# Entry of layer 1: queries and first keys built tile by tile of the contraction, values ahead of the context's keys, norms placed anew

## The chip, the cores and the metric

One core of a Trainium2 chip runs the whole forward pass as one program. The metric is the device time of one execution in microseconds (us). Three runs of the kernel before took 1241.14, 1241.52 and 1244.07 us; the median is 1241.52.

TensorE (PE) multiplies, VectorE (DVE) and ScalarE (ACT) work on tiles, GpSimd (POOL) takes small element-wise work, and the queue of SyncE (SP) issues nearly all DMAs.

## The reference, cut to what matters

Two layers act on 256 latent and 256 context tokens of width 1024. Layer 0 is retention, layer 1 differential attention; each ends in a gated feed-forward net. Every sublayer starts with an RMS norm whose result is scaled and shifted by vectors computed from a condition ("adaLN"). In the last layer only the latent tokens are wanted, so layer 1 forms queries for latents alone, but keys and values for both streams.

```python
h = rms_norm(x) * (1.0 + scale) + shift          # for latents and for context
q, k, v = split(h @ w_in)                        # width 1024 each, 8 heads x 2 x 64
q, k = rms_norm_gain(q), rms_norm_gain(k)        # over each 64; rope_2d on the latents' only
s = q @ k.T / 8                                  # two score maps m per head
p = softmax(s[m=0]) - lam * softmax(s[m=1])
o = rms_norm_gain(p @ v) * (1 - lambda_init)     # over each 128
x = x + gate * (o @ w_out)
```

All of it is float32.

## The kernel before

**Streams.** `xs[m]`, `hh[m]`, `hl[m]` hold feature tile m (128 features, m = 0 to 7) of all 512 tokens: columns 0 to 255 are the context (`CTX`), 256 to 511 the latents (`LAT`). Every float32 product is done as three products of a high and a low part in the rounded type `fp32r` (`mm3`, L106): high x high, high x low, low x high. `split` (L102) makes the parts: ACT copies to the high one, DVE subtracts to the low one. Weights are loaded and split by `load_w` (L113) in pieces of 128 x 1024; each of the rings `raw`, `whi`, `wlo` has five buffers. One load of 1024 rows by 256 columns is two such pieces, contraction tiles 0 to 3 and 4 to 7.

**Order.** Each engine runs its instructions in one fixed order. The framework fixes it when the program is built: among what it expects to be ready by its own costs, the instruction written first goes first, so a matmul written later can be put ahead of one whose operands it expects late. Two lists place work in the written order. `after(n, fn)` (L70) runs `fn` at the n-th coming `step()`, and `acc()` (L83), which hands out one of four accumulator banks, begins with a `step()`. In layer 1 `defer(n, fn)` (L755) runs `fn` at the n-th coming `tick()`; a tick stands behind each half projection (24 matmuls of 128 x 256).

**End of layer 0.** `ffn_out` (L675) adds the last part of the feed-forward net: eight blocks of 12 matmuls for the latents, then eight for the context. `gated_add` (L308) adds each block to `xs` on DVE, ACT squares the result, and POOL adds the square to a running sum (`norm_square`, L272). The sum over features is then taken by four small matmuls, and DVE and POOL form the inverse root (`norm`, L291). Its `spread` brings the root to all partitions by matmuls against `ones` (L249), and `modulate` (L257) makes `hh`, `hl`: per tile one DVE instruction, one on ACT and one more on DVE. `NB` and `NS` (L42, L44) say how many steps later the norm and its spread are run: for the latents 0 and 6, for the context 0 and 0. The context's are thus written ahead of the first query matmul, in the `acc()` of that projection.

**Layer 1.** Four groups g of two heads (`diff_group`, L816). The written order of group 0 is: queries of the latents, keys of the latents, keys of the context, values of the latents (token tiles 2, 3), values of the context (0, 1). `proj_pair` (L767) forms 128 tokens x 256 columns of one token tile over all eight contraction tiles, then the next token tile, both in one bank. `qk_pair` (L778) squares on ACT, sums on DVE, takes the root on POOL, multiplies by it, and applies gain and rope on DVE. Transposes on PE (`q_transpose`, `k_transpose`) are deferred by `PQK` ticks; the tile of scores (`scores`), the transposed probabilities (`probs`) and the products with the values (`values`) by `SC0` + `STEP0` in group 0 and `SC` + `STEP` in groups 1 and 2. The scores have two banks of their own (tag `sc`, one buffer of two banks), the transposes two (tag `tp`).

Of the kernel before, what the change touches and what calls it, by code (L numbers as in the profile page):

```python
# [11 lines left out]
F32 = mybir.dt.float32  # L12
F32R = mybir.dt.float32r
AF = mybir.ActivationFunctionType
ALU = mybir.AluOpType
AX = mybir.AxisListType

P = 128
# [32 lines left out]
def hybrid_trunk(ctx: ExitStack, tc: tile.TileContext, xt_in, cols_in, ada_first, ada_wt, c, c_ctx, ret_w_in,  # L51
# [18 lines left out]
    def after(n, fn):  # L70
        queue.append([n, fn])
# [219 lines left out]
    def norm(layer, which, half, a, later):  # L291
        nm = f"{layer}_{which}_{half.start}"
        ps = tps(f"ms_{nm}")
        for i in range(2):
            T.matmul(ps[:, 2 * i:2 * i + 2], a[:, i * P:(i + 1) * P], mean_col, start=True, stop=True)
        rc = small.tile([P, 2], F32, tag="rc", name=f"rc_{nm}")
        V.tensor_copy(rc, ps[:, 0:4:2])
        rsqrt(rc)

        def spread():  # L300
            r, = spread_rows(rc, nm)
            for m in range(KT):
                modulate(layer, which, m, half, r)
            fresh[half.start] = (layer, which)

        after(later, spread)

    def gated_add(layer, ch, m, half, ps):  # L308
        s = 0 if half == CTX else 1
# [221 lines left out]
    for h in range(NH0):  # L531
        us = [None] * 4

        def u_hook(i):
            for j in range(4):
                if UP[j] == i:
                    us[j] = ret_u(h - 1, j, pend[0], pend[1][j])

        q, k, *sgs = ret_first() if h == 0 else ret_qk(h, u_hook)
        if h == 0:  # L540
            V.tensor_scalar(out=lw[:, 4], in0=lw[:, 3], scalar1=2.0, scalar2=None, op0=ALU.add)
            V.reciprocal(lw[:, 5], lw[:, 4])
            V.tensor_tensor(out=lw[:, 4], in0=lw[:, 3], in1=lw[:, 5], op=ALU.mult)
            V.tensor_tensor(out=lw[:, 5], in0=lw[:, 4], in1=lw[:, 4], op=ALU.mult)
            V.tensor_scalar(out=lw[:, 6], in0=lw[:, 5], scalar1=1.0 / 19, scalar2=1.0 / 17, op0=ALU.mult, op1=ALU.add)
            for kk in (15, 13, 11, 9, 7, 5, 3, 1):
                V.tensor_tensor(out=lw[:, 6], in0=lw[:, 6], in1=lw[:, 5], op=ALU.mult)
                V.tensor_scalar(out=lw[:, 6], in0=lw[:, 6], scalar1=1.0 / kk, scalar2=None, op0=ALU.add)
            V.tensor_tensor(out=lw[:, 6], in0=lw[:, 6], in1=lw[:, 4], op=ALU.mult)
            V.tensor_scalar(out=lw[:, 7], in0=lgt, scalar1=0.0, scalar2=None, op0=ALU.min)  # L550
            V.scalar_tensor_tensor(out=lg, in0=lw[:, 6], scalar=-2.0, in1=lw[:, 7], op0=ALU.mult, op1=ALU.add)

            lgn = loc.tile([P, 8], F32, name="lgn")
            V.tensor_scalar(out=lgn, in0=lg, scalar1=float(NL), scalar2=None, op0=ALU.mult)
            lneg = loc.tile([P, 8], F32, name="lneg")
            V.tensor_scalar(out=lneg, in0=lg, scalar1=-1.0, scalar2=None, op0=ALU.mult)
            lam4 = scratch("lam4")[:, :4 * DH].rearrange("p (a d) -> p a d", a=4)
            nc.sync.dma_start(lam4.rearrange("p a d -> p (a d)"),
                              diff_lambda.rearrange("o a d -> o (a d)").broadcast_to([P, 4 * DH]))
            lam = const.tile([P, 8], F32, name="lam")  # L560
            lv = scratch("lv")[:, :2 * DH].rearrange("p (a d) -> p a d", a=2)
            V.tensor_tensor(out=lv[:, 0], in0=lam4[:, 0], in1=lam4[:, 1], op=ALU.mult)
            V.tensor_tensor(out=lv[:, 1], in0=lam4[:, 2], in1=lam4[:, 3], op=ALU.mult)
            V.tensor_reduce(out=lam[:, 0:2], in_=lv, op=ALU.add, axis=AX.X)
            S.activation(lam[:, 2:4], lam[:, 0:2], AF.Exp)
            V.tensor_tensor(out=lam[:, 4:5], in0=lam[:, 3:4], in1=lam[:, 2:3], op=ALU.subtract)
            V.tensor_scalar(out=lam[:, 5:6], in0=lam[:, 4:5], scalar1=-LAMBDA_INIT, scalar2=None, op0=ALU.add)
            neg_lam = lam[:, 5:6]
            fs = decay_tables(0)
        if pend is not None:  # L570
            ret_out(h - 1, us, [ALL])
        pt = ret_scores(h, q, k, fs)
        vs = ret_v(h)
        sgs = sgs[0] if sgs else ret_g(h, 0)
        os = ret_av(h, pt, vs)
        if h + 1 < NH0:
            fs = decay_tables(h + 1)
        us = [None] * 4

        def u_last(i):  # L580
            for j in range(4):
                if UL[j] == i:
                    us[j] = ret_u(h, j, os, (sgs + done)[j])

        done = []
        sgs += ret_g(h, 1, u_last if h == NH0 - 1 else None, done)
        pend = (os, sgs)
    ret_out(NH0 - 1, us, [CTX, LAT])

    def ffn_in(layer, g0, g1, first):  # L590
# [84 lines left out]
    def ffn_out(layer, g0, g1, us, done=None):  # L675
# [14 lines left out]
        if layer == 0:  # L690
            for half in ([LAT, CTX] if g1 == 4 else [ALL]):
                n = half.stop - half.start
                a = None
                for m in range(KT):
                    ps = acc(f"fo_{layer}_{g0}_{m}_{half.start}")
                    mm3(ps[:, :n], [wv(m, k) + (us[k][0][:, half], us[k][1][:, half]) for k in range(g1)])
                    if n == NT:
                        gated_add(0, 5, m, CTX, ps[:, CTX])
                        gated_add(0, 5, m, LAT, ps[:, LAT])
                    else:  # L700
                        gated_add(0, 5, m, half, ps[:, :n])
                        a = norm_square(1, 0, half, m, a)
                if n == NL:
                    after(NB[2 + (half == CTX)], lambda half=half, a=a: norm(1, 0, half, a, NS[2 + (half == CTX)]))
        else:
            for m0 in range(0, KT, 2):
                ps = acc(f"fo_{layer}_{g0}_{m0}")
                for m in (m0, m0 + 1):
                    mm3(ps[:, (m - m0) * NL:(m - m0 + 1) * NL], [wv(m, k) + us[k] for k in range(g1)])
                for m in (m0, m0 + 1):  # L710
                    gated_add(1, 5, m, LAT, ps[:, (m - m0) * NL:(m - m0 + 1) * NL])
                    if done is not None:
                        done(m)
# [61 lines left out]
                tick()  # L775
        return ps

    def qk_pair(w, wt, t0, name):  # L778
        ps = proj_pair(wt, t0, name)
        sq = scratch(f"sq_{name}")  # L780
        S.activation(sq, ps, AF.Square)
        ss = small.tile([P, 8], F32, tag="ss", name=f"ss_{name}")
        V.tensor_reduce(out=ss, in_=sq.rearrange("p (g i) -> p g i", g=8), op=ALU.add, axis=AX.X)
        rsqrt(ss, EPS * DH)
        n = loc.tile([P, 512], F32, tag="qkn", name=f"n_{name}", bufs=2)
        nv = n.rearrange("p (g i) -> p g i", g=8)
        V.tensor_tensor(out=nv, in0=ps.rearrange("p (g i) -> p g i", g=8),
                        in1=ss.unsqueeze(2).broadcast_to([P, 8, DH]), op=ALU.mult)
        o = loc.tile([P, 512], F32, tag="qko", name=f"o_{name}", bufs=2)
        if t0 < 2:  # L790
            V.tensor_tensor(out=o.rearrange("p (g i) -> p g i", g=8), in0=nv,
# [24 lines left out]
    def diff_group(g):  # L816
# [27 lines left out]
                V.tensor_tensor(out=k2[m][b, :, dst], in0=tv[a], in1=k2[m][a, :, dst].bitcast(F32), op=ALU.subtract)  # L844
            st["k", t0] = k2

        qo = qk_pair(0, wq, 2, f"q_{g}")
        tick()
        defer(PQK[0 if g else 2], lambda: q_transpose(qo))
        for t0 in (2, 0):  # L850
            ko = qk_pair(1, wk, t0, f"k_{g}_{t0}")
            tick()
            defer(PQK[1 if g else 3 + (t0 == 0)], lambda t0=t0, ko=ko: k_transpose(t0, ko))
        wv = load_w(wi1[:, 2048 + g * 256:2048 + (g + 1) * 256], KT, 256, f"dv_{g}")
        v = loc.tile([P, 4, 256], F32, tag="v1", name=f"v1_{g}", bufs=2)

# [50 lines left out]
        def heads_out():  # L907
# [8 lines left out]
                                   op0=ALU.mult, op1=ALU.subtract)  # L916
            st["out"] = (hi, lo)

        for n, (i, h) in enumerate(((0, 0), (0, 1), (1, 0), (1, 1))):
            at = (SC0 if g == 0 else SC if g < 3 else SC3)[n]  # L920
            for k, fn in enumerate((scores, probs, values)):
                defer(at + (STEP0 if g == 0 else STEP if g < 3 else STEP3)[k], lambda fn=fn, i=i, h=h: fn(i, h))
        defer((HO if g < 3 else HO3)[0], heads_out)
        for n in range(4):
            defer((HO if g < 3 else HO3)[1 + n], lambda n=n: diff_out(g, st, 2 * n))
        def value_half(t):
            if t % 2 == 0:
                st["vps", t // 2] = acc(f"ps_dv_{g}_{t}")
            ts, half = slice(t * P, (t + 1) * P), slice((t % 2) * 256, (t % 2 + 1) * 256)
            ps = st["vps", t // 2]  # L930
            mm3(ps[:, half], [(hh[k][:, ts], hl[k][:, ts], wv[0][k], wv[1][k]) for k in range(KT)])
            if t % 2:
                S.activation(v[:, t - 1:t + 1].rearrange("p t n -> p (t n)"), ps, AF.Copy)
                st["v", t // 2] = v

        for n, t in enumerate((2, 3, 0, 1)):
            if g < 3:
                value_half(t)
                tick()
            else:  # L940
                defer(V3[n], lambda t=t: value_half(t))
# [108 lines left out]
```

## Time and profile before

| | |
|---|---|
| median of three runs | 1241.52 us |
| profiled execution, its own time | 1245.21 us |
| its span, first to last instruction | 1243.4 us |
| mean granted share of PE's clock | 0.995 |
| PE busy | 1207.1 us, 97% |
| weight loads into PE | 1045.8 us, 84% |
| DVE busy | 852.5 us, 69% |
| ACT busy | 471.0 us, 38% |
| POOL busy | 84.3 us, 7% |
| HBM read | 174.14 MB, 141 GB/s over the span |
| chain that ended last, by engine | PE 84%, DVE 8%, POOL 3%, ACT 2%, issue 2%, DMA 1% |

The profile is of one execution. Busy time counts the instructions of an engine from start to end; PE's overlap one another, and a row with `[idle before <-releaser]` says how long the engine stood still and what it then waited for. In names, buffer numbers are left out: `ps_q`, `ps_k`, `ps_dv` are the projections of layer 1, `sqa` the running sum of squares, `ms` its sum over features, `rb` the spread root, `qtp`, `ktp`, `ptp` transposes of queries, keys and probabilities, `dsc` scores.

### The profile page before, as it was taken

Reading aid. Unit: us, or ns where it says so; the run is one execution under the profiler, and the core shown is the slowest. Engines: PE = TensorE matmul, PEld = TensorE weight load, DVE = VectorE, ACT = ScalarE, POOL = GpSimd, SP = SyncE. Lnnn points to the kernel's source line nnn. Section 1 sums busy time; section 2 is a strip of 40 time slices with the busy share of each in tenths; the row PEclk is TensorE's granted clock in tenths of the full one; section 3 lists DMA queues with packets and bytes.
Section 4 is the critical chain, followed back from the end, with each engine's and each line's share of the span. In section 5 each row is a group of like instructions: output and inputs, shape, how many; then the busy total and the mean of one; then the engine's idle time right before and its main releaser. Section 6 shows DMA issues by size and latency. Waiting matters only on the chain.

```text
span 1243.4 us, 18122 instructions
## 1 busy us (share of the span) xinstructions
PE 1207.1 (97%) x7136; PEld 1045.8 (84%) x7136; DVE 852.5 (69%) x1483; ACT 471.0 (38%) x756; POOL 84.3 (7%) x87
## 2 busy tenths in 40 slices
PE   6999999999999999999999999999899998999998
PEld 5677778878788788888888888888899998999998
DVE  3479896688597579976575543348787788855555
ACT  3253323224232235323222312225565566644442
POOL 0000000000000032000000000012212112000000
PEclk9999999999999999999999999999999999999999
DMA  9724455245344332766576532232222413657563
GB/s 315 269 83 128 154 161 156 82 125 155 95 124 156 98 105 70 236 206 193 180 234 187 165 123 76 94 102 86 85 87 68 119 35 102 181 183 212 158 184 102
DMA packets 127509, 176.36 MB, mean 142 GB/s; under 512 B 6721, under 2 KB 100417, under 8 KB 127425
## 3 DMA queue, kind: packets, MB, share of 16 engines
q1 hardware_dynamic: 126272, 174.42, 45.2%
q8 instruction: 56, 0.92, 0.3%
q10 hardware_dynamic: 1152, 0.79, 0.2%
q14 instruction: 29, 0.23, 0.1%
HBM read 174.14 MB, written 1.05 MB: 141 GB/s over the span
## 4 chain that ended last, share of the span: by engine, by line
PE 84%; DVE 8%; POOL 3%; ACT 2%; issue 2%; DMA 1%; POOLq 0%; ACTq 0%; DVEq 0%
PE fo L111 5%; PE fo L110 5%; PE fo L109 5%; PE fpg L111 5%; PE fpg L109 5%; PE fpg L110 5%; PE fpa L111 5%; PE fpa L109 5%; PE fpa L110 5%; PE vps L109 2%; PE vps L111 2%; PE vps L110 2%; PE gps L110 2%; PE gps L111 2%; PE gps L109 2%; PE qkps L109 2%
## 5 line engine op out<-in xcount | busy, mean ns | idle before, releaser
L230 DVE CUSTOM_DVE_ANT_0 junk<-adaw,silb,biasx 128x1024 bf16<-128x1024 f32 x128 | 165.1, 1290 | 58.4 <-DMA adaw<-in_ada_wt_dram 57.7
L109 PE MATMUL fo<-fuh,whi_fo 128*128 128x256 f32 (+1 forms) x352 | 115.1, 327 | 0.0
L110 PE MATMUL fo<-ful,whi_fo 128*128 128x256 f32 (+1 forms) x352 | 114.9, 326 | 0.0
L111 PE MATMUL fo<-fuh,wlo_fo 128*128 128x256 f32 (+1 forms) x352 | 114.9, 326 | 0.0
L104 DVE TENSOR_TENSOR wlo_fo<-raw_fo,whi_fo 128x1024 fp32r<-128x1024 f32 (+1 forms) x56 | 55.6, 994 | 59.5 <-ACT whi_fo L103 59.4
L103 ACT ACTIVATE whi_fo<-raw_fo 128x1024 fp32r<-128x1024 f32 (+1 forms) x56 | 49.1, 878 | 113.5 <-PE fo L110 62.3
L109 PE MATMUL fpa<-hh,whi_fa 128*128 128x512 f32 (+1 forms) x192 | 72.6, 378 | 1.1 <-ACT hh L266 1.1
L110 PE MATMUL fpg<-hl,whi_fg 128*128 128x512 f32 (+1 forms) x192 | 72.6, 378 | 0.0
L109 PE MATMUL fpg<-hh,whi_fg 128*128 128x512 f32 (+1 forms) x192 | 72.5, 378 | 0.0
L110 PE MATMUL fpa<-hl,whi_fa 128*128 128x512 f32 (+1 forms) x192 | 72.5, 378 | 0.0
L111 PE MATMUL fpa<-hh,wlo_fa 128*128 128x512 f32 (+1 forms) x192 | 72.5, 377 | 0.0
L111 PE MATMUL fpg<-hh,wlo_fg 128*128 128x512 f32 (+1 forms) x192 | 72.4, 377 | 0.0
L109 PEld LDWEIGHTS fo<-fuh,whi_fo 128*128 128x128 f32 x352 | 66.1, 188 | 6.7
L110 PEld LDWEIGHTS fo<-ful,whi_fo 128*128 128x128 f32 x352 | 66.1, 188 | 6.7
L111 PEld LDWEIGHTS fo<-fuh,wlo_fo 128*128 128x128 f32 x352 | 66.1, 188 | 6.6
L311 DVE SCALAR_TENSOR_TENSOR x<-fo,mod,x 128x256 f32<-128x256 f32 x96 | 42.8, 479 | 40.7 <-PE fo L111 40.7
L104 DVE TENSOR_TENSOR wlo_fg<-raw_fg,whi_fg 128x1024 fp32r<-128x1024 f32 x40 | 49.0, 1226 | 29.9 <-ACT whi_fg L103 29.9
L279 POOL TENSOR_TENSOR sqa<-sqa,sq 128x256 f32<-128x256 f32 x35 | 35.6, 1017 | 396.2 <-issue 346.9
L103 ACT ACTIVATE whi_fa<-raw_fa 128x1024 fp32r<-128x1024 f32 x40 | 42.3, 1057 | 51.9 <-PE fo L110 18.9
L104 DVE TENSOR_TENSOR wlo_fa<-raw_fa,whi_fa 128x1024 fp32r<-128x1024 f32 x40 | 48.7, 1221 | 17.2 <-ACT whi_fa L103 16.7
L103 ACT ACTIVATE whi_fg<-raw_fg 128x1024 fp32r<-128x1024 f32 x40 | 42.4, 1060 | 45.0 <-issue 14.7
L109 PE MATMUL ops<-uh,whi_wo 128*128 128x512 f32 (+1 forms) x160 | 56.4, 364 | 1.4 <-ACT uh L103 1.1
(315 smaller groups left out, 3475.3 us busy)
## 6 DMA issues: line engine op xcount, KB each, us to landing
adaw<-in_ada_wt_dram SPq DMA_DIRECT2D x80, 512.0 KB, 3.7
raw_fa<-in_ffn_w_in_dram SPq DMA_DIRECT2D x40, 512.0 KB, 3.6
raw_fg<-in_ffn_w_in_dram SPq DMA_DIRECT2D x40, 512.0 KB, 4.3
raw_fo<-in_ffn_w_out_dram SPq DMA_DIRECT2D x32, 512.0 KB, 3.5
ada<-in_ada_first_dram SPq DMA_DIRECT2D x32, 256.0 KB, 5.4
raw_v<-in_ret_w_in_dram SPq DMA_DIRECT2D x16, 512.0 KB, 3.7
raw_wo<-in_ret_w_out_dram SPq DMA_DIRECT2D x16, 512.0 KB, 3.8
raw_g<-in_ret_w_in_dram SPq DMA_DIRECT2D x14, 512.0 KB, 3.6
```

Source lines behind the costliest of these rows:

```text
L103: S.activation(hi, src, AF.Copy)
L104: (eng or V).tensor_tensor(out=lo, in0=src, in1=hi.bitcast(F32), op=ALU.subtract)
L109: T.matmul(out_ps, ah, bh, start=(first and i == 0), stop=False)
L110: T.matmul(out_ps, ah, bl, start=False, stop=False)
L111: T.matmul(out_ps, al, bh, start=False, stop=(last and i == n - 1))
L230: V.tensor_tensor_reduce(out=junk, in0=raw, in1=silb[:, s], scale=1.0, scalar=biasx[:, b:b + 1], op0=ALU.mult, op1=ALU.add, accum_out=mod[ ...
L279: G.tensor_tensor(out=a, in0=a, in1=sq, op=ALU.add)
L311: V.scalar_tensor_tensor(out=xs[m][:, half], in0=ps, scalar=mod[:, layer, ch, s, m:m + 1], in1=xs[m][:, half], op0=ALU.mult, op1=ALU.add)
```

## The change

The opening of group 0 goes over the contraction tiles outermost: for each k three products, queries of token tile 2, queries of tile 3, first keys of tile 2, in three banks (the queries' two are the score banks). The context's norm is written into step 3 and its spread into step 6 of that loop. The second half of the latent keys follows, then the latent values, then the context's keys, and only then are the scores deferred. At the end of layer 0 the latents' norm and its spread are now run 2 and 2 steps later.

```diff
@@ norm
-        after(later, spread)
+        if isinstance(later, dict):
+            later["spread"] = spread
+        else:
+            after(later, spread)
@@ ahead of ret_out of the last head
+    sq0 = [None]
     ret_out(NH0 - 1, us, [CTX, LAT])
@@ ffn_out, layer 0
-                if n == NL:
-                    after(NB[2 + (half == CTX)], lambda half=half, a=a: norm(1, 0, half, a, NS[2 + (half == CTX)]))
+                if n == NL and half == LAT:
+                    after(2, lambda half=half, a=a: norm(1, 0, half, a, 2))
+                elif n == NL:
+                    sq0.append(a)
@@ layer 1
-    def qk_pair(w, wt, t0, name):
-        ps = proj_pair(wt, t0, name)
+    chain = {}
+
+    def opening(wq, wk):
+        ps = apsum.tile([P, 2, 512], F32, tag="sc", name="ps_q_open")
+        pk = acc("ps_k_open")
+        need(1, 0, LAT)
+        for k in range(KT):
+            if k == 3:
+                norm(1, 0, CTX, sq0[1], chain)
+            if k == 6:
+                chain["spread"]()
+            for o, t, w in ((ps[:, 0, :256], 2, wq), (ps[:, 1, :256], 3, wq), (pk[:, :256], 2, wk)):
+                ts = slice(t * P, (t + 1) * P)
+                mm3(o, [(hh[k][:, ts], hl[k][:, ts], w[0][k], w[1][k])], k == 0, k == KT - 1)
+        tick()
+        return ps[:, :, :256], pk
+
+    def opening_key(pk, wk):
+        ts = slice(3 * P, 4 * P)
+        mm3(pk[:, 256:], [(hh[k][:, ts], hl[k][:, ts], wk[0][k], wk[1][k]) for k in range(KT)])
+        tick()
+        return pk
+
+    def qk_pair(w, wt, t0, name, ps=None):
+        ps = proj_pair(wt, t0, name) if ps is None else ps
...
@@ diff_group
-        qo = qk_pair(0, wq, 2, f"q_{g}")
+        pq, pk = (None, None) if g else opening(wq, wk)
+        qo = qk_pair(0, wq, 2, f"q_{g}", pq)
         tick()
         defer(PQK[0 if g else 2], lambda: q_transpose(qo))
-        for t0 in (2, 0):
-            ko = qk_pair(1, wk, t0, f"k_{g}_{t0}")
+        ko = qk_pair(1, wk, 2, f"k_{g}_2", None if g else opening_key(pk, wk))
+        tick()
+        defer(PQK[1 if g else 3], lambda ko=ko: k_transpose(2, ko))
+
+        def context_keys():
+            ko = qk_pair(1, wk, 0, f"k_{g}_0")
             tick()
-            defer(PQK[1 if g else 3 + (t0 == 0)], lambda t0=t0, ko=ko: k_transpose(t0, ko))
+            defer(PQK[1 if g else 4], lambda: k_transpose(0, ko))
+
+        if g:
+            context_keys()
...
+        if g == 0:
+            for t in (2, 3):
+                value_half(t)
+                tick()
+            context_keys()
         for n, (i, h) in enumerate(((0, 0), (0, 1), (1, 0), (1, 1))):
             at = (SC0 if g == 0 else SC if g < 3 else SC3)[n]
...
-        for n, t in enumerate((2, 3, 0, 1)):
+        for n, t in enumerate((2, 3, 0, 1) if g else (0, 1)):
             if g < 3:
                 value_half(t)
                 tick()
```

In `qk_pair` the squares and the products with the root read the queries of group 0 from two banks through views of one more dimension; `value_half` moves up unchanged, with a check of its operands.

## Rows read from the trace of the kernel before

**Rows 1.** Windows: us, busy us (instructions) by engine, PE clock, DMA share, GB/s.

```profile
850.20:861.00 10.80, 8.44 (x62) 7.42 (x60) 9.56 (x22) 5.80 (x11) 3.01 (x3) 1.00 0.29 89
861.00:875.62 14.62, 13.77 (x111) 13.54 (x112) 12.89 (x31) 8.52 (x15) 2.54 (x1) 1.00 0.35 108
875.62:889.10 13.48, 10.69 (x87) 10.32 (x88) 10.64 (x20) 7.00 (x11) 4.18 (x2) 1.00 0.25 79
889.10:928.50 39.40, 38.87 (x310) 37.78 (x309) 34.14 (x58) 24.25 (x50) 6.49 (x4) 1.00 0.28 81
```

**Rows 2.** Waits of PE, 850.2 to 863: waited for, total, times, longest us.

```profile
PE ps_q L109 <- ACT hh L266: 0.9, 2, 0.5
```

**Rows 3.** Timeline of PE, 838 to 905: start, length, instruction, times, idle before.

```profile
839.37 0.61 PE L295 MATMUL ms<-mean_col,sqa 128*128 128x2 f32 x4 [0.56 <-POOL sqa L279]
...
846.98 0.59 PE L249 MATMUL rb<-dg,ones 128*128 128x256 f32 x2
...
851.73 0.28 PE L109 MATMUL ps_k<-whi_dk,hh 128*128 128x256 f32 x1
...
856.23 0.28 PE L110 MATMUL ps_q<-wlo_dq,hh 128*128 128x256 f32 x1
857.72 0.61 PE L295 MATMUL ms<-mean_col,sqa 128*128 128x2 f32 x4 [1.21 <-POOL sqa L279]
...
861.10 0.70 PE L249 MATMUL rb<-dg,ones 128*128 128x256 f32 x2 [0.27 <-DVE dg L246]
```

**Rows 4.** Waits of PE, 863 to 892.

```profile
PE ktp L813 <- DVE o_k L805: 1.5, 1, 1.5
PE ktp L813 <- DVE ql L833: 1.3, 1, 1.3
PE qtp L813 <- issue: 0.8, 1, 0.8
```

**Rows 5.** Window in layer 1's first feed-forward stage, four banks; PE alone.

```profile
1066.00:1078.00 12.00, 12.00 (x102) 1.00 0.36 110
```

**Rows 6.** Groups of DVE, 843.9 to 858: times, busy us, mean ns, idle before.

```profile
L265 DVE SCALAR_TENSOR_TENSOR n<-x,mod,r 128x256 f32<-128x256 f32 x8 | 4.0, 546 | 0.0
L267 DVE SCALAR_TENSOR_TENSOR hl<-n,mod,hh 128x256 fp32r<-128x256 f32 x8 | 3.9, 531 | 0.0
...
L311 DVE SCALAR_TENSOR_TENSOR x<-fo,mod,x 128x256 f32<-128x256 f32 x5 | 2.4, 476 | 0.9 <-PE fo L111 0.9
```

**Rows 7.** Timeline of DVE, 838 to 905.

```profile
848.43 1.84 DVE L265 SCALAR_TENSOR_TENSOR n<-x,mod,r 128x256 f32<-128x256 f32 x3
...
855.34 0.47 DVE L311 SCALAR_TENSOR_TENSOR x<-fo,mod,x 128x256 f32<-128x256 f32 x1
...
857.01 0.94 DVE L267 SCALAR_TENSOR_TENSOR hl<-n,mod,hh 128x256 fp32r<-128x256 f32 x1
...
861.60 1.23 DVE L104 TENSOR_TENSOR wlo_dv<-raw_dv,whi_dv 128x1024 fp32r<-128x1024 f32 x1 [0.56 <-ACT whi_dv L103]
```

**Rows 8.** Timeline of POOL, 838 to 905.

```profile
838.59 0.72 POOL L279 TENSOR_TENSOR sqa<-sqa,sq 128x256 f32<-128x256 f32 x1 [0.66 <-ACT sq L277]
...
856.49 1.18 POOL L279 TENSOR_TENSOR sqa<-sqa,sq 128x256 f32<-128x256 f32 x1 [0.48 <-ACT sq L277]
```

**Rows 9.** Timeline of ACT, 838 to 905.

```profile
860.51 1.06 ACT L103 ACTIVATE whi_dv<-raw_dv 128x1024 fp32r<-128x1024 f32 x1 [4.17 <-PE ps_q L111]
...
895.63 0.20 ACT L871 ACTIVATION_READ_ACCUMULATOR p<-dsc,mx 128x1 f32 x1
```

**Rows 10.** Timeline of DVE, the first keys' chain.

```profile
878.26 0.69 DVE L787 TENSOR_TENSOR n_k<-ps_k,ss_k 128x512 f32<-128x512 f32 x1 [1.53 <-POOL ss_k L143]
```

**Rows 11.** Timeline of PE at scores and transposed probabilities.

```profile
892.00 0.39 PE L864 MATMUL dsc<-k,qh 128*128 128x512 f32 x1
...
945.17 0.63 PE L881 MATMUL ptp<-ident,pf 128*128 128x128 f32 x4 [0.96 <-DVE pf L874]
...
992.47 0.63 PE L881 MATMUL ptp<-ident,pf 128*128 128x128 f32 x4 [1.86 <-DVE pf L874]
```

More of the change, by code (lines that the diff above doesn't have):

```diff
@@ L776, in proj_pair @@
         return ps
-    def qk_pair(w, wt, t0, name):
-        ps = proj_pair(wt, t0, name)
-        sq = scratch(f"sq_{name}")
-        S.activation(sq, ps, AF.Square)
+    chain = {}
[20 more added lines that the diff above has]
+        ps = proj_pair(wt, t0, name) if ps is None else ps
+        sq = scratch(f"sq_{name}")
+        if len(ps.shape) == 3:
+            S.activation(sq.rearrange("p (t n) -> p t n", t=2), ps, AF.Square)
+            ps = ps.rearrange("p t (g i) -> p t g i", g=4)
+        else:
+            S.activation(sq, ps, AF.Square)
+            ps = ps.rearrange("p (t g i) -> p t g i", t=2, g=4)
         ss = small.tile([P, 8], F32, tag="ss", name=f"ss_{name}")
@@ L786, in qk_pair @@
         nv = n.rearrange("p (g i) -> p g i", g=8)
-        V.tensor_tensor(out=nv, in0=ps.rearrange("p (g i) -> p g i", g=8),
-                        in1=ss.unsqueeze(2).broadcast_to([P, 8, DH]), op=ALU.mult)
+        V.tensor_tensor(out=n.rearrange("p (t g i) -> p t g i", t=2, g=4), in0=ps,
+                        in1=ss.rearrange("p (t g) -> p t g", t=2).unsqueeze(3).broadcast_to([P, 2, 4, DH]), op=ALU.mult)
         o = loc.tile([P, 512], F32, tag="qko", name=f"o_{name}", bufs=2)
@@ L917, in heads_out, with value_half @@
             st["out"] = (hi, lo)
+        def value_half(t):
+            if t % 2 == 0:
+                st["vps", t // 2] = acc(f"ps_dv_{g}_{t}")
+            ts, half = slice(t * P, (t + 1) * P), slice((t % 2) * 256, (t % 2 + 1) * 256)
+            ps = st["vps", t // 2]
+            need(1, 0, LAT if t >= 2 else CTX)
+            mm3(ps[:, half], [(hh[k][:, ts], hl[k][:, ts], wv[0][k], wv[1][k]) for k in range(KT)])
+            if t % 2:
+                S.activation(v[:, t - 1:t + 1].rearrange("p t n -> p (t n)"), ps, AF.Copy)
+                st["v", t // 2] = v
+        if g == 0:
[3 more added lines that the diff above has]
+            context_keys()
         for n, (i, h) in enumerate(((0, 0), (0, 1), (1, 0), (1, 1))):
@@ L925, in diff_group @@
             defer((HO if g < 3 else HO3)[1 + n], lambda n=n: diff_out(g, st, 2 * n))
[L926 to L934, printed above, removed]
-        for n, t in enumerate((2, 3, 0, 1)):
+        for n, t in enumerate((2, 3, 0, 1) if g else (0, 1)):
             if g < 3:
```

## The prediction

> **What bounds the kernel now.** TensorE (PE) is busy 97% of the span, so time can only come from where it stands still. I read the stretches of the entry of layer 1 first. From 850.20, where the first query matmul starts, to 889.10, where group 0's last value matmul ends, PE is busy 32.9 of 38.9 us, and VectorE (DVE) 33.1 of 38.9 [rows 1]: PE has 6.0 us of gaps beside a DVE that is 85% full. In the next 39.4 us PE lacks 0.5 us. Then the waits of PE inside it. Up to 863 they are 0.9 us for `hh` (the latent stream just normalised) [rows 2], 1.21 us for the sum of squares of the context half, and 0.27 us for its spreading matmul [rows 3]. After 863 they are 0.8, 1.5 and 1.3 us at the transposes of queries and keys [rows 4]. These six sum to 6.0 us, all of the gaps. The order on PE shows why they are where they are: six key matmuls stand at 851.73 in the middle of the query's [rows 3]. The framework orders each engine at build time, by the order written and by what it expects to be ready; PE then follows that order, and waits where DVE, ACT or POOL are later than expected. So the kernel already fills part of its `hh` waits with keys, and what is left are errors of that expectation.
>
> **The change, part by part.** The sum is made against the profiled execution, 1245.2 us: a span of 1243.4 and 1.8 around it that nothing here touches. That is 3.7 us above the median of 1241.52; I carry the difference over to the median.
>
> Matmuls: none is added or removed. The opening has 8 x 9 = 72, the rest of the first keys 24, together the 96 that queries and first keys have now. Contraction-outer over several banks costs no pitch: the first feed-forward stage of layer 1 runs so over four banks, with 102 matmuls in 12.00 us and no gap [rows 5], 0.118 us each. Weights loaded into PE are as many as before. Cost 0; bounds 0 and 96 x 0.118 x 1%, 0.1 us.
>
> `hh` waits (0.9 us): now one query half uses up a `hh` tile every 3 matmuls, 0.35 us. DVE makes one in (4.0 + 3.9) / 8 = 0.99 us [rows 6]. The opening takes 9 matmuls per tile, 1.06 us, so supply keeps pace even if it only starts together with PE. It starts earlier. The latent spreading matmul stands at 846.98, five blocks of 12 matmuls behind the sums at 839.37 [rows 3]. Written as 2 and 2, the norm stays behind block 0, where it stands already, and the spread comes two blocks later and so three blocks earlier than now: 846.98 - 36 x 0.118 = 842.7. The same chain for the context half took 861.10 - 857.72 = 3.4 us [rows 3], which would be 842.8: no wait, or 0.1. The first modulation, at 848.43 now [rows 7], starts at about 844.2. I take -0.9; bounds -0.9 and 0.
>
> Context sums (1.21 us): the last gated add of the context half starts at 855.34, because the latent modulation is ahead of it on DVE [rows 7]; the last POOL add ends at 857.67 and PE's sum starts at 857.72 [rows 8, 3]. From the start of that add to the sum are 2.3 us. Modulation 7.9 us and five gated adds 2.4 us [rows 6] from 844.2 end at 854.5 if nothing goes between, so the last add starts at 854.0 and the sum is ready at 856.3; with one weight split of 1.2 us [rows 7] between, at 857.5, hardly earlier than now. If the add goes ahead of the modulation, when its matmuls end near 850.5, the sum is ready at 852.8. PE asks for it after 27 opening matmuls, 850.2 + 3.2 = 853.4: a wait of 0, 2.9 or 4.1 us, less what the framework sees coming and fills with later matmuls, as it did with the keys. I take half of 2.9 as filled, a wait of 1.5, hence +0.3; bounds -1.2 and +2.9. What is queued behind it on PE is the opening itself, and nobody waits for that before the query chain.
>
> At this place the row shows more: a POOL add takes 0.72 us at 838.59 and 1.18 us at 856.49, beside which one DVE `hl` took 0.94 us [rows 8, 7], against a mean of 0.53 [rows 6]. The Trainium skill, page "SBUF — State Buffer", section "Who interferes with whom", says that a DVE instruction with two SBUF inputs contends with a GpSimd instruction that reads SBUF, as an exclusive lock; the trace agrees (0.72 against 1.18). By that rule the earlier modulation puts more of the context adds beside it, some 0.4 us each, which speaks against the change and for the dear end of this term.
>
> Spread of the context half (0.27 us): 27 matmuls, 3.2 us, now lie between sum and spread, against a chain of 3.4: -0.2; bounds -0.3 and +0.3. The second half of the key weights and the values': the split of the second value half waits for the query weights' buffer until 860.51 [rows 9]; the opening gives that buffer up after its fourth step, near 854.5 plus the wait, so it comes earlier, behind a latent value projection that starts only at 850.2 + 96 x 0.118 = 861.5. Key weights of steps 4 to 7 are split after the context half ends and are needed at 854.5; DVE may be late by about one split, 1.2 us, but beside the wait above: 0, bounds 0 and +1.2. Banks: queries leave the four accumulator banks for the two that the scores use first at about 890, so nothing is taken away.
>
> Transposes (0.8 + 1.5 + 1.3 us): in matmuls the due points of queries (144) and first keys (168) stay. The queries' chain on DVE hangs on the context modulation, which ends about as much earlier as the spread does; PE comes earlier too. I take -0.3 of 0.8. The first keys now leave PE right behind the queries, with 48 value matmuls between them and the context keys, so that their turn on POOL runs beside the queries' chain: the 1.53 us that DVE stood still for it at 878.26 [rows 10] should go, hence -1.2 of the 1.5. The context keys' transpose moves from matmul 216 to 264 (5.6 us), past the `ql` copy that it waited for: -1.3. Together -2.8; bounds -3.6 and 0.
>
> Scores of group 0: they are deferred two steps later, because the clock stands at 8 and not at 6 when they are written; their first is due at matmul 312, not 264, their fourth at step 20, where group 1's first is due as well. No work is added, but one score bank goes round in 895.83 - 892.00 = 3.8 us [rows 9, 11], and probabilities that come late already stop PE for 0.96 and 1.86 us where several due points coincide [rows 11]. Later projections can fill. I take +0.9, one such wait; bounds 0 and +5.6, two in each of two groups. The split weights of group 0's output are held two steps longer too, past the start of group 3's keys. The last key split then takes the buffer of group 3's first query tile, free 12 matmuls before the keys start and needed 12 after that: 2.8 us for an ACT and a DVE split of 1.06 + 1.23 [rows 9, 7]; 0, bounds 0 and +1.2.
>
> Sum: -0.9 + 0.3 - 0.2 + 0 - 2.8 + 0.9 = -2.7. Engine idle undercounts a gap on PE by the tail of the matmul before it: from 856.23 to 857.72 are 1.49 us from start to start, less one pitch 1.37, where the row says 1.21 [rows 3]. Five gaps closed or nearly so add 5 x 0.16 = 0.8. That gives **-3.5 us**: 1241.7 in the frame of the profiled execution, **1238.0** against the median.
>
> **Rivals.** (A) The waits only move. DVE is 85% full through the entry [rows 1]; if its work ends when it ends now, the transposes wait as before and only the `hh` waits turn into a longer wait for the context sums: -0.9 - 0.2 + 2.0 - 0.9 (some of the keys' transposes) = 0.0, 1241.5. For it: the sum above has the context's gated adds hardly earlier. Against it: the DVE gap of 1.53 us and the `ql` wait are matters of order, not of work. The change would also not do all it says, as the framework interleaves queries and keys already [rows 3].
>
> (B) Everything comes in time: all 6.0 us of gaps, the six tails (1.0) and the 0.96 of [rows 11] go: -8.0, 1233.5. For it: the 48 matmuls that PE gains ahead of the scores. Against it: the context sums.
>
> (C) Slower, by the scores. If group 0's four tiles and group 1's four share the one score bank from step 13 to 28 and each of group 1's waits in PE's order for late probabilities, that is 4 x 1.86 = 7.4 us, where the entry gives back 3.5 + 0.9 = 4.4: +3.0, 1244.5; with the key split late as well, +4.2. It decides the sign from the third such wait on. For it: 1.86 us at 992.47 [rows 11]. Against it: in 889.10 to 928.50, where these tiles run now, PE lacks 0.5 us [rows 1], so there is room to fill.
>
> **How the numbers follow.** Forecast 0.55, A 0.22, B 0.10, C 0.13. Less than 0.3%, 3.7 us, can't be told from no change. The forecast's own range is -6.5 to -0.5 (1235.0 to 1241.0); its middle lies at the bound, so its 0.55 goes 0.28 to faster and 0.27 to same. B is faster (0.10); A is same, but for 0.02 each way (0.18, 0.02, 0.02); C is slower in 0.07 and same in 0.06. Faster 0.40, same 0.51, slower 0.09. The range from 1233.0 to 1244.0 leaves out the far half of B and of C, and the ends of the forecast.
>
> **What would show it.** Right: no PE wait for `hh` after 850; latent modulation from about 844; a PE wait for the context sums of 1 to 3 us in the opening; queries' transpose with a wait under 0.6 us and no wait at the context keys'. Wrong: PE gaps of more than 4 us between the opening and the end of group 0's values (A); more than two waits for `pf` or `p` above 0.9 us between 890 and 972 (C); no wait at the context sums at all (B).

## The result and the profile after

The changed kernel is slower: a median of 1255.85 us (four runs, 1254.61 to 1256.54) beside 1242.77 for the kernel before (four runs, 1241.14 to 1244.07), a ratio of 1.0092 with a 95% interval of 1.0079 to 1.0106, some 11.4 us. Ratios here and below are those on record, over fast runs alone (one run of c_free, 5349.57 us, is left out); the plain quotient of the two medians above is 1.0105, 13.1 us. 1238.0 was forecast, in a range from 1233 to 1244. The profiled execution took 1255.67 us, 10.5 more than the profiled one of before; PE is busy for 1211.1 us of its span of 1253.9, again 97%, and DVE (VectorE) for 853.3.

Where it went is seen first in windows cut at PE's own marks: first query matmul of group 0, of group 1, of group 2, of group 3, and first matmul of the feed-forward net. Columns as in [rows 1]. Before:

```profile
850.22:889.12 38.90, 32.90 (x260) 31.28 (x259) 33.09 (x71) 21.32 (x36) 9.73 (x6) 1.00 0.30 92
889.12:928.53 39.41, 38.88 (x310) 37.76 (x309) 34.15 (x58) 24.28 (x50) 6.49 (x4) 1.00 0.28 81
928.53:972.52 43.99, 43.03 (x350) 41.90 (x348) 34.77 (x64) 24.55 (x54) 7.48 (x5) 1.00 0.24 73
972.52:1051.56 79.04, 73.64 (x565) 69.63 (x564) 66.16 (x130) 47.32 (x113) 12.73 (x10) 0.98 0.31 94
```

After:

```profile
851.88:891.24 39.36, 32.89 (x256) 32.07 (x255) 31.57 (x61) 18.14 (x31) 12.60 (x9) 0.96 0.27 81
891.24:933.28 42.04, 39.13 (x311) 37.56 (x309) 33.03 (x58) 24.40 (x47) 8.16 (x5) 1.00 0.34 101
933.28:982.16 48.88, 46.39 (x353) 44.31 (x352) 37.05 (x67) 25.19 (x60) 8.01 (x5) 0.97 0.22 66
982.16:1061.32 79.16, 73.93 (x565) 69.71 (x564) 66.26 (x128) 47.05 (x112) 11.85 (x10) 0.98 0.30 94
```

The entry itself, the stretch that I argued about, is 0.5 us longer. Group 1's stretch lost 2.6 and group 2's 4.9 us, places to which the prediction gave 0.9 together. These are 8.1 of the 10.5 us. Of the rest, 1.7 lies ahead of 839, in layer 0 (the latent sums stand at 841.09, not 839.37), and 0.7 behind 1061. Both come and go among the runs below by more than that, also in kernels that share this code, so I don't put them to the change; what is left of them in the median is open.

The entry has the same length but another inside. Waits of PE from 851 to 892 (waited for, total, times, longest), which answer to [rows 2, 4]:

```profile
PE ms L295 <- POOL sqa L279: 3.4, 1, 3.4
PE ktp L847 <- DVE o_k L839: 1.5, 1, 1.5
PE qtp L847 <- issue: 1.3, 1, 1.3
PE ps_k_open L109 <- DVE x L314: 0.3, 1, 0.3
```

The `hh` waits are gone. The wait for the context sums (`ms`) is 3.39 us where it was 1.21 [rows 3], and the transposes wait as they did: 1.34 for queries, 1.48 for the first keys, and 1.18 for the context's keys, now at 895.46 and so counted in the next window. That hides a part of the loss: with its matmuls this transpose takes an estimated 1.9 us across the border (the entry of ov_late is so much shorter than that of o_late, below), so the entry lost about 2.4 us and group 1's stretch about 0.7. PE's timeline at the sums and at the spread, and later in group 2's stretch:

```profile
858.55 0.61 PE L295 MATMUL ms<-mean_col,sqa 128*128 128x2 f32 x4 [3.39 <-POOL sqa L279]
...
859.34 0.28 PE L111 MATMUL ps_q_open<-whi_dq,hl 128*128 128x256 f32 x1
859.46 0.28 PE L109 MATMUL ps_q_open<-whi_dq,hh 128*128 128x256 f32 x1
...
861.00 0.41 PE L110 MATMUL ps_k_open<-wlo_dk,hh 128*128 128x256 f32 x1
861.21 0.41 PE L111 MATMUL ps_k_open<-whi_dk,hl 128*128 128x256 f32 x1
...
866.09 0.59 PE L249 MATMUL rb<-dg,ones 128*128 128x256 f32 x2
...
961.64 0.63 PE L923 MATMUL ptp<-ident,pf 128*128 128x128 f32 x4 [1.85 <-DVE dst L142]
```

Behind the 3.39 us the matmuls follow each other by 0.12 us at first (859.34, 859.46), and from 860.17 by 0.21 (861.00, 861.21), until 863.56. The granted clock (third column from the end) says why:

```profile
855.00:859.00 4.00, 0.61 (x6) 0.45 (x5) 4.00 (x3) 0.69 (x1) 3.34 (x3) 1.00 0.37 113
859.00:861.00 2.00, 2.00 (x15) 2.00 (x15) 2.00 (x5) 1.06 (x1) 0.06 (x1) 0.80 0.80 219
861.00:864.00 3.00, 3.00 (x17) 3.00 (x17) 1.47 (x3) 0.00 (x0) 1.55 (x1) 0.57 0.88 252
864.00:868.00 4.00, 4.00 (x34) 3.95 (x34) 0.86 (x3) 1.28 (x3) 0.00 (x0) 1.00 0.73 248
...
962.00:966.00 4.00, 4.00 (x20) 3.73 (x19) 3.38 (x7) 2.73 (x4) 1.88 (x2) 0.57 0.43 131
```

PE did little from 855 to 859, then ran at the lower level, 1.2 GHz, for some 3.4 us: 16 matmuls at a distance of 0.21 in place of 0.118 are 1.5 us more. The same stands behind the 1.85 us at 961.64. Neither is in the trace of before, whose lowered clock falls once in these stretches, at 1044.

Why the sums are late is in POOL's and DVE's timeline [rows 7, 8]:

```profile
845.50 2.23 DVE L265 SCALAR_TENSOR_TENSOR n<-x,mod,r 128x256 f32<-128x256 f32 x4 [0.36 <-ACT r L253]
...
852.39 1.65 DVE L314 SCALAR_TENSOR_TENSOR x<-fo,mod,x 128x256 f32<-128x256 f32 x4
...
854.50 1.75 DVE L104 TENSOR_TENSOR wlo_dq<-raw_dq,whi_dq 128x1024 fp32r<-128x1024 f32 x1
856.18 3.40 DVE L104 TENSOR_TENSOR wlo_dk<-raw_dk,whi_dk 128x1024 fp32r<-128x1024 f32 x2
...
859.57 1.21 DVE L104 TENSOR_TENSOR wlo_dv<-raw_dv,whi_dv 128x1024 fp32r<-128x1024 f32 x1
```

```profile
851.89 1.17 POOL L279 TENSOR_TENSOR sqa<-sqa,sq 128x256 f32<-128x256 f32 x1 [5.24 <-ACT sq L277]
853.55 4.95 POOL L279 TENSOR_TENSOR sqa<-sqa,sq 128x256 f32<-128x256 f32 x4 [0.49 <-ACT sq L277]
```

The latent modulation starts three blocks earlier, as foreseen, and holds back the context's last gated adds: four stand in a row at 852.39. Their squares then go through POOL one behind the other beside three weight splits: 1.24 us for an add (0.72 alone, [rows 8]) and 1.70 to 1.75 for a split (the row of 3.40 us is two; 1.21 at 859.57, with POOL idle). This is the contention for which the prediction cited the Trainium skill ("SBUF — State Buffer", "Who interferes with whom"); the trace agrees, and shows that both sides pay. The last add ends at 858.50, 6.6 us behind the first query matmul, where it was 7.5 before (857.67 against 850.22). So the sums do come 0.8 us earlier; but PE asks for them 3.0 us earlier: after 3.3 us, where it was 6.3.

### The profile page after: what moved, and what is told of

The parts are those of the page before. It is cut to its first block, busy times and chain, and to the rows that moved or that the text cites. A ratio compares the mean times of both kernels' runs of the same rounds, so it can differ in the third digit from the quotient of the medians.

```text
span 1253.9 us, 18127 instructions
## 1 busy us (share of the span) xinstructions
PE 1211.1 (97%) x7136; PEld 1048.2 (84%) x7136; DVE 853.3 (68%) x1483; ACT 469.5 (37%) x756; POOL 84.6 (7%) x87
## 4 chain that ended last, share of the span: by engine, by line
PE 77%; DVE 12%; POOL 4%; issue 3%; ACT 3%; DMA 2%; POOLq 0%; ACTq 0%; DVEq 0%; SPq 0%
PE fo L109 5%; PE fo L111 5%; PE fo L110 5%; PE fpa L109 5%; PE fpg L109 5%; PE fpa L111 5%; PE fpg L111 5%; PE fpg L110 5%; PE fpa L110 5%; PE gps L110 2%; PE gps L111 2%; PE gps L109 2%; PE qkps L109 2%; PE vps L109 2%; PE qkps L110 2%
```

## Experiments

Twelve kernels, each compared with the kernel before on its chip. Short names below: T is the deferral of group 0's scores, probabilities, values and outputs two ticks later; O the opening with the moved norms; V the latent values ahead of the context's keys. A table at the end of this part has all stretches.

**1. Later scores alone (t_late), and taken out of the change (ov_early).** In t_late:

```diff
-SC0 = (5, 6, 8, 12)
+SC0 = (7, 8, 10, 14)
-        defer(HO[0], heads_out)            # group 0
+        defer(HO[0] + 2, heads_out)        # and the four diff_out likewise
```

ov_early is the changed kernel with group 0's due points put back where they were:

```diff
-SC0 = (5, 6, 8, 12)
+SC0 = (3, 4, 6, 10)
-        defer(HO[0], heads_out)            # group 0
+        defer(HO[0] - 2, heads_out)        # and the four diff_out likewise
```

> The kernel before with one edit: group 0's scores, probabilities, values and output products are due two steps later; opening, norms and the order of the projections stay as before. Theory S (most of the loss comes from the later scores of group 0, which then bunch with group 1's): 4 to 7 us slower than before, with new PE waits at transposed probabilities or at the queries' and keys' transposes of groups 1 and 2 after 890, and the entry up to 889 unchanged. Rival N (the loss comes from the context norm asked for inside the opening, with PE's clock lowered after that wait): within 1 us of before.

> The changed kernel with group 0's scores, probabilities, values and output products due two steps earlier, that is at the steps of before (the first at 11). Theory S: 4 to 7 us faster than the changed kernel, so 4 to 7 us above before. Theory N: within 1 us of the changed kernel, about 11 us above before.

t_late: 1.0051 (1.0035 to 1.0067). ov_early: 1.0045 (1.0020 to 1.0070), against 1.0092 with T. So T costs half a per cent both added and taken out, some 6 us: the largest part of the loss. The windows of t_late, of groups 1 and 2 and of the half clock, have it where the changed kernel has it, 0.7 and 5.1 us longer than before:

```profile
889.88:929.98 40.10, 38.49 (x307) 37.12 (x305) 31.64 (x55) 23.23 (x45) 6.55 (x4) 1.00 0.27 79
929.98:979.08 49.10, 46.61 (x354) 44.28 (x352) 37.05 (x67) 25.19 (x60) 8.03 (x5) 0.97 0.22 65
959.70:963.10 3.40, 3.40 (x15) 3.08 (x15) 3.03 (x6) 2.10 (x3) 1.28 (x2) 0.50 0.51 154
```

and ov_early's windows of groups 1 and 2 are 44.24 and 43.99: group 2 is as before. Counted on PE, four matmuls of scores (0.86 us) moved from group 1's stretch to group 2's. Without them group 1's lost 1.5 us, all in one wait of 1.6 at a query transpose. Group 2's lost 4.3: 1.5 in waits, some 1.5 to 1.7 by the half clock (the third row); the rest, in small gaps, I did not itemise. The wait in t_late (930 to 980) is the one of the changed kernel at 961.64:

```profile
PE ptp L881 <- DVE dst L142: 1.9, 1, 1.9
...
```

**2. Which part of T: scores (sc_late) or outputs (ho_late).** sc_late has only the first edit above, ho_late only the second.

> The kernel before with only group 0's scores, probabilities and values due two steps later; its output transposes and products stay due at the steps of before. Theory S1 (the cost of the later steps comes from the scores, which meet group 1's): 4 to 6 us slower than before. Theory S2 (it comes from the output transposes, which then stand beside group 1's probabilities in the fourth quarter of the stage): within 1.5 us of before.

> The kernel before with only group 0's output transposes and output products due two steps later; scores, probabilities and values stay. Theory S1: within 1.5 us of before. Theory S2: 4 to 6 us slower than before, with the wait of about 1.9 us behind the output transposes in group 2's part and PE's clock lowered behind it.

sc_late: 1.0063 (1.0044 to 1.0081); ho_late: 1.0002 (0.9990 to 1.0015). It is the scores. With the outputs left early (sc_late), the waits of group 2's stretch stand at them, and not at `ptp`, but the length is the same (49.53) and the clock halves again behind them (949.9 to 953.3):

```profile
PE ontp L912 <- DVE on L903: 2.5, 2, 1.4
PE dops L109 <- ACT doh L914: 0.5, 1, 0.5
...
```

So the late tile of scores pushes one chain (score, probability, value, output) into group 2, and PE waits at whichever of its members is due first. That is a reading of these two traces; what orders it so within the framework I did not trace.

**3. The opening in parts: with its norms (o_only), without (c_only), the latents' norm alone (n_lat).** o_only is the changed kernel with the order of the values, and so the due points, as before:

```diff
-        if g:
-            context_keys()
+        context_keys()
...
-        if g == 0:
-            for t in (2, 3):
-                value_half(t)
-                tick()
-            context_keys()
...
-        for n, t in enumerate((2, 3, 0, 1) if g else (0, 1)):
+        for n, t in enumerate((2, 3, 0, 1)):
```

c_only is o_only with the norms as before:

```diff
-                if n == NL and half == LAT:
-                    after(2, lambda half=half, a=a: norm(1, 0, half, a, 2))
-                elif n == NL:
-                    sq0.append(a)
+                if n == NL:
+                    after(NB[2 + (half == CTX)], lambda half=half, a=a: norm(1, 0, half, a, NS[2 + (half == CTX)]))
...
-            if k == 3:
-                norm(1, 0, CTX, sq0[1], chain)
-            if k == 6:
-                chain["spread"]()
```

n_lat is the kernel before with

```diff
-NB = (3, 0, 0, 0)
+NB = (3, 0, 2, 0)
-NS = (3, 0, 6, 0)
+NS = (3, 0, 2, 0)
```

> The changed kernel with the order of before for keys and values: queries and first keys contraction-outer with the context norm at step 3, its spread at step 6, and the latent norm at 2 and 2, but context keys ahead of the values, so that the scores are due at the steps of before. Theory N: 4 to 6 us slower than before, with the wait of 3.4 us for the context sums and the lowered clock behind it as in the changed kernel. Theory S: within 1.5 us of before, since the entry of the changed kernel cost only 0.7 us more than that of before.

> The kernel before with the contraction-outer opening alone: norms written where the kernel before has them (latents 0 and 6, context ahead of the opening), projections in the order of before. Theory N: the waits for the normalised latents go (0.9 us) and the context sums are met late enough, so 1 to 3 us faster than before. Rival D (DVE sets the end of the entry whatever the order on PE): within 1 us of before, the wait moving to the transposes.

> The kernel before with the latents' norm and spread 2 and 2 steps later alone, nothing else. Theory L: the early spread takes the 0.9 us of waits for the normalised latents, but holds the context's gated adds back on DVE, so that the wait for the context sums, asked for ahead of the queries, grows from 1.2 to 2 to 4 us: 0 to 3 us slower than before. Rival: 1 to 2 us faster.

o_only: 1.0031 (1.0012 to 1.0049); c_only: 1.0008 (0.9991 to 1.0024); n_lat: 1.0038 (1.0020 to 1.0055). The contraction-outer order alone does nothing to the time that can be told from noise; the norms as placed make it slower, and the latents' does so without the new opening. Waits of PE in c_only's entry:

```profile
PE ktp L841 <- DVE ql L861: 1.4, 1, 1.4
PE ktp L841 <- DVE o_k L833: 1.3, 1, 1.3
PE qtp L841 <- issue: 1.2, 1, 1.2
PE ps_k_open L110 <- DVE wlo_dk L104: 0.7, 1, 0.7
...
```

No `hh`, no `ms`: this entry is 37.59 us, 1.3 shorter, but the next stretch is 41.12, 1.7 longer. In n_lat and o_only the longest wait is the one of the changed kernel, 3.63 and 3.39 us at `ms`, and the half clock stands behind it: 6.8 us of it in n_lat, 3.4 in o_only.

```profile
855.12 1.01 PE L295 MATMUL ms<-mean_col,sqa 128*128 128x2 f32 x4 [3.63 <-POOL sqa L279]
```

(n_lat.) Counted on PE, the sums stand behind 36 matmuls of queries and keys in the kernel before, behind 52 in c_only, behind 14 in n_lat and behind 22 in the changed kernel, although all but the last have them written ahead of the first. So the framework does put later matmuls ahead of them; with the latents' norm early, the one thing in which n_lat differs from before, it puts fewer.

**4. The context's norm later (o_late), with the latents' as before (o_late_l06), and less work on DVE (c_free).** o_late is o_only with

```diff
-            if k == 3:
+            if k == 6:
                 norm(1, 0, CTX, sq0[1], chain)
-            if k == 6:
-                chain["spread"]()
             for o, t, w in (...):
                 ...
+        chain["spread"]()
         tick()
```

o_late_l06 is o_late with the latents' norm as before:

```diff
-                    after(2, lambda half=half, a=a: norm(1, 0, half, a, 2))
+                    after(0, lambda half=half, a=a: norm(1, 0, half, a, 6))
```

c_free is c_only with fewer splits in `load_w`, for the value weights of group 0 and the query and key weights of group 1:

```diff
-            split(raw[:, :n], hi[:, :n], lo[:, :n], eng)
+            if low:
+                split(raw[:, :n], hi[:, :n], lo[:, :n], eng)
+            else:
+                S.activation(hi[:, :n], raw[:, :n], AF.Copy)
+                lo = hi
```

Where `low` is false, the low part is not formed and the high part stands in its place; PE has the same matmuls. From the entry to the feed-forward net DVE is busy 161.8 us, where c_only has 168.1.

> The run with the opening alone (contraction-outer, latent norm at 2 and 2, context keys ahead of the values), with one edit: the context norm is written into step 6 of the opening and not step 3, its spread behind step 7 and not into step 6. Theory N (the opening costs 3.9 us because it asks 3.4 us too early for the context sums, after which the clock is low): the wait for the sums under 0.5 us, no low clock near 860, 3 to 5 us faster than the opening alone. Rival D (DVE sets the end of the entry): the wait goes, but the transposes wait longer; 0 to 2 us faster than the opening alone.

> The opening alone with the late context norm, and the latents' norm back at 0 and 6 steps, as before has it. Theory L (the early latent spread is what lets the opening run without waiting for its tiles): the waits for the normalised latents come back, 1 to 3 us slower than with 2 and 2. Rival (the opening uses tiles slowly enough anyway): within 1 us.

> The contraction-outer opening with the norms of before, and five weight splits less on DVE between 850 and 890 (the low parts of group 0's value weights and of group 1's query and key weights are not computed; the high part stands in their place, so the numbers of those products are wrong and their work on PE is the same). 6 us of DVE work are gone. Rival D (DVE's load makes PE wait in the entry): the waits at the three transposes, 3.95 us with the splits, fall under 1.5 us, and it is 3 to 5 us faster than with them. Rival P (the waits are errors of the plan, which shortens with the work): they stay between 2.5 and 4 us, within 2 us of the time with the splits.

o_late: 0.9966 (0.9948 to 0.9985), median 1240.01: faster than both kernels. o_late_l06: 1.0003 (0.9985 to 1.0021). c_free: 0.9973 (0.9961 to 0.9985). One edit, asking for the sums three steps later (and for their spread behind the loop), is worth 0.65%, some 8 us, between o_only and o_late; of that the profiled executions show 4.8 us in the entry, and 1.6 in the last stretch, where the half clock falls more often in o_only's. Waits in o_late's entry, its sums (behind 54 matmuls, without a wait), and its clock:

```profile
PE ktp L846 <- DVE o_k L838: 1.4, 1, 1.4
PE ktp L846 <- DVE o_k L824: 1.2, 1, 1.2
PE ps_q_open L110 <- DVE wlo_dq L104: 0.7, 1, 0.7
...
```

```profile
858.85 0.50 PE L295 MATMUL ms<-mean_col,sqa 128*128 128x2 f32 x4
```

```profile
850.00:858.00 8.00, 6.73 (x51) 5.97 (x49) 8.00 (x11) 4.73 (x9) 5.90 (x5) 1.00 0.23 69
858.00:866.00 8.00, 7.87 (x62) 7.61 (x63) 6.83 (x15) 3.13 (x6) 3.40 (x2) 1.00 0.86 274
```

Neither the wait nor the half clock is there, although nothing on POOL got faster. Its four adds in a row take 4.96 us, as in the changed kernel:

```profile
851.80 4.96 POOL L279 TENSOR_TENSOR sqa<-sqa,sq 128x256 f32<-128x256 f32 x4 [0.48 <-ACT sq L277]
...
862.89 2.70 POOL L143 TENSOR_TENSOR ss_q<-ss_q,neg_half 128x8 f32<-128x8 f32 x1 [1.71 <-DVE ss_q L142]
```

The queries' transpose does not wait any more either. Their root on POOL (`ss_q`) is asked for at 862.89, ahead of the context's modulation on DVE and beside it; in the changed kernel it ran at 873.92, behind the modulation, and DVE stood still for it:

```profile
868.73 0.68 DVE L817 TENSOR_REDUCE ss_q<-sq_q 128x8 f32<-128x512 f32 x1
873.67 0.17 DVE L142 TENSOR_SCALAR ss_q<-ss_q 128x8 f32<-128x8 f32 x1
876.49 0.69 DVE L821 TENSOR_TENSOR n_q<-ps_q_open,ss_q 128x512 f32<-128x512 f32 x1 [1.13 <-POOL ss_q L143]
...
881.75 0.69 DVE L821 TENSOR_TENSOR n_k<-ps_k_open,ss_k 128x512 f32<-128x512 f32 x1 [1.75 <-POOL ss_k L143]
```

(the changed kernel again). o_late_l06 says that the latents' early norm is needed too: without it the stretches are those of c_only. The reason is not the one expected: no wait for `hh` comes back, but the waits at the three transposes do (1.2, 1.3 and 1.4 us). c_free asks whether the transposes wait because DVE is full. Its time came out as D had it, 0.35% below c_only, its waits as P had it, 2.8 us. Of c_only's three such waits one is gone (`ql`), and the other two are no shorter:

```profile
PE ktp L845 <- DVE o_k L837: 1.5, 1, 1.5
PE qtp L845 <- issue: 1.3, 1, 1.3
```

So less work on DVE took away that one, and the 1.7 us in the next stretch (39.44 here). Whether the load itself does it isn't shown: the framework also made another order of it, with the spread's matmul behind 61 matmuls of the opening and not 76. The other two do not yield to less work on DVE; that leaves the chain's own length and the place of the transposes in PE's order, argued and not shown for the keys' one.

**5. The values' order, and T once more, on the late norm (ov_late, after_late).** Both take the edit of o_late: ov_late is ov_early with it, after_late the changed kernel with it.

> The same, with group 0's scores, probabilities, values and outputs due two steps earlier, at the steps of before. If the order of values and context keys costs nothing of itself: 3 to 5 us faster than before, like the late norm with context keys first. Rival V (with the scores due as before, the context keys' transpose, 48 matmuls later, is on the path to the first scores): 0 to 4 us slower than before.

> The changed kernel with one edit: the context norm written into step 6 and not 3, its spread behind step 7. If the parts add up (norms 3.9 + 4.2 us between the opening with the norm at step 3 and at step 6, later scores 6 us): 5 to 8 us faster than the changed kernel, so 3 to 6 us above before. Rival (the value order makes its own loss, with the context keys' transposes late): less than 4 us faster.

ov_late: 0.9992 (0.9975 to 1.0008); after_late: 1.0018 (1.0005 to 1.0031). From o_late to ov_late V costs 0.26%, from ov_late to after_late T costs 0.26%; the intervals of each pair overlap a little. With the faulty norm V cost 0.14% (o_only to ov_early), which those intervals can't tell from nothing. V's place is group 1's stretch, 44.36 in ov_late for 39.45 in o_late, where its entry is 1.9 shorter: the context keys' transpose (a wait of 1.3 and its matmuls) crosses the border, and `ptp` and `ktp` wait for 0.9 and 0.6; the rest of the 4.9 us, in small gaps, I did not itemise. T here takes some of that back (42.18), which fits its smaller price on this base.

All stretches, in us, from such windows (one profiled execution each; 1.5 to 2 us of the last one is a half clock that falls there in some runs and not in others; the entries of ov_early and n_lat hold 6.8 us at half clock, where that of the changed kernel holds 3.4, and that of ho_late holds 3.4 as well):

| kernel | ratio | entry | group 1 | group 2 | group 3, rest | sum |
|---|---|---|---|---|---|---|
| before | 1 | 38.90 | 39.41 | 43.99 | 79.04 | 201.3 |
| changed | 1.0092 | 39.36 | 42.04 | 48.88 | 79.16 | 209.4 |
| t_late | 1.0051 | 38.95 | 40.10 | 49.10 | 79.18 | 207.3 |
| sc_late | 1.0063 | 38.91 | 40.10 | 49.53 | 79.43 | 208.0 |
| ho_late | 1.0002 | 39.90 | 39.44 | 45.26 | 79.09 | 203.7 |
| ov_early | 1.0045 | 40.84 | 44.24 | 43.99 | 79.15 | 208.2 |
| o_only | 1.0031 | 41.42 | 39.43 | 43.98 | 81.03 | 205.9 |
| c_only | 1.0008 | 37.59 | 41.12 | 44.00 | 81.01 | 203.7 |
| n_lat | 1.0038 | 42.70 | 39.41 | 44.01 | 77.90 | 204.0 |
| o_late | 0.9966 | 36.64 | 39.45 | 44.00 | 79.41 | 199.5 |
| o_late_l06 | 1.0003 | 37.60 | 41.14 | 44.00 | 80.96 | 203.7 |
| c_free | 0.9973 | 36.81 | 39.44 | 43.99 | 79.28 | 199.5 |
| ov_late | 0.9992 | 34.71 | 44.36 | 43.98 | 77.88 | 200.9 |
| after_late | 1.0018 | 34.71 | 42.18 | 48.77 | 78.86 | 204.5 |

The parts add up: O 0.31%, T 0.51% and V 0.14% make 0.96%, and 0.92% was measured, each within some 0.2%.

## Why the prediction was wrong, step by step

- **Matmuls, 0:** right. Away from the half clock the opening runs at 0.12 us a matmul.
- **`hh` waits, -0.9:** right; none is left, and the modulation starts 4.4 us behind the latent sums (845.50 against 841.09), where 4.8 was worked out.
- **Context sums, +0.3: failed.** The working gave them ready 2.6, 6.1 or 7.3 us behind the first query matmul, and PE asking after 3.2. Measured: ready after 6.6, asked for after 3.3. The middle branch was right to half a us, and its wait of 2.9 (3.39 measured) stood in the text. The step that failed is "I take half of 2.9 as filled": PE has 22 opening matmuls ahead of the sums, not more than the 27 that the loop wrote there, and the wait was paid whole. The runs fit a framework that expects the sums too soon once the latents' norm is early (n_lat: 14 matmuls ahead, a wait of 3.63 us; the kernel before: 36 and 1.21 us); its own costs were not read. What was not in the sum at all is the clock: the wait is paid again, by 1.5 us, in matmuls at 1.2 GHz. Together +2.2 and +1.5 for the +0.3; o_late, which differs from o_only in this place alone, shows 4.8 us in the entry (41.42 to 36.64), the queries' transpose included.
- **Spread, -0.2; key split, 0:** right; no wait at `rb` (866.09), 0.3 us at `ps_k_open` in all. The split was late, but beside the wait for the sums, as was said: in o_late, without that wait, two splits make PE wait for 0.7 and 0.3 us.
- **Transposes, -2.8: failed.** They wait for 4.0 us, where it was 3.6. The step was that the first keys' turn on POOL runs beside the queries' chain. DVE takes its work in one order: the keys' squares are summed only within the queries' chain (878.63), their root is asked for behind it (880.08), and DVE then stands still for 1.75 us, where it was 1.53 [rows 10]. c_free shows that one wait of the three goes with less work on DVE, o_late that the queries' is one of order and goes when their root is taken ahead of the context's modulation.
- **Scores, +0.9: failed, by size.** About +6 measured alone (medians 6.0 in t_late, 5.9 in sc_late), at the bound of 5.6 or past it. The bound was made of waits only; some 1.5 us of what was measured is the half clock behind such a wait. The value taken, one wait, rested on "later projections can fill"; it held neither in group 1, where one wait of 1.6 us appeared, nor in group 2.
- **Tails, -0.8:** fell with the waits that stayed; three gaps closed (two at `hh`, one at the spread), not five.
- **The values' order** had no term but the transposes' gain. Its own price is between nothing and some 3 us.

Of its signs the first two came (no wait for `hh`, the early modulation); the wait for the sums, at 3.39 us, is over its 1 to 3, and both signs at the transposes failed. Of the rivals, A describes the opening without its norms (c_only: waits moved, the time the same), though not by the wait that it named. C had the sign and the mechanism, bunched scores, but not the place: it foresaw four waits of 1.86 for probabilities in group 1, and there was one of 1.6 at a query transpose there and one of 1.85 in group 2, with the clock behind it. Its condition (from the third wait on) was set by a gain in the entry that never came.

## What to carry to other kernels

When a wait is moved, work out for both places when it is ready and when it is asked for. An earlier producer is worth nothing to a consumer that moves up further: the sums came 0.8 us earlier, were asked for 3.0 us earlier, and the opening lost 0.31%, which three loop steps' delay turned into a gain of 0.34%. Do not count on the framework to fill a wait that its own costs do not foresee: look where it placed the consumer and how many matmuls it put ahead (36 before, 14 in n_lat). And a deferral counted in steps shifts when other work is put ahead of it; check what is due beside it two stages on, since that is where the bill came.

## What the hardware showed that was not expected

- A stop of PE can be paid twice. In the changed kernel, behind 3.39 us of standing, the clock fell to 1.2 GHz 1.6 us after PE had resumed, and stayed there for 3.4 us (1.5 us lost); in ov_early and n_lat it was low already when PE resumed, and stayed so until 6.8 us had passed. Behind single waits of 1.85 and 1.86 us it did so at 962 in the changed kernel and at 993.5 in c_only, but not at 992.47 in the kernel before [rows 11], where the granted clock from 992.50 to 996.00 is 1.00. Nor do the same waits in the same order decide it: ho_late's opening waits as that of before (0.55, 0.32 and 1.21 us), and behind the 1.21 us its clock was at 1.2 GHz for 3.4 us, while before, t_late and sc_late show 1.00 there. Where PE stood for 3.39 or 3.63 us it fell in all four traces that have them, and in none of the six with a contraction-outer opening and no wait for the sums. So it can't be told from the length of one wait. What decides is left open, and 1.5 us behind a stop is a risk, not a fixed price.
- POOL's adds and DVE's weight splits slow each other by 70% and 40% (0.72 to 1.24 us, 1.21 to 1.70). The prediction had a row for DVE's side (0.94 for 0.53), but no price for it in the sum.
